# Samples' weighted sums as products of 256 columns, and a second quad in the planned entry of a feed-forward layer

## Chip, cores and metric

One core of a Trainium2 chip runs the whole program. The metric is device time in microseconds, the median of several executions. Engines are named as in the profile: PE (TensorE matmul) and PEld (its weight loads), DVE (VectorE), ACT (ScalarE), POOL (GpSimd), SP (SyncE, which issues the DMAs).

## The reference

A trunk of two layers runs over 1024 prompt rows and 64 sample rows (8 batches of 8 new tokens), width 1024. Layer 0 mixes tokens with a gated MLP, layer 1 with sliding-window attention; each is followed by a SwiGLU feed-forward layer of width 2816. The samples' attention reads cached keys and values:

```python
kk = jnp.concatenate([cache_k.astype(k_new.dtype), k_new], axis=1)
vv = jnp.concatenate([cache_v.astype(v_new.dtype), v_new], axis=1)
...
probs = sink_softmax(scores, sinks.reshape(N_KV_HEADS, Q_PER_KV))
out = jnp.einsum('bkgts,bskd->btkgd', probs.astype(vv.dtype), vv)
...
return (jax.nn.silu(h @ w_gate) * (h @ w_up)) @ w_down
```

For each sample batch b and key head k, 8 query heads x 8 tokens are weighted sums over 128 cached and 8 new value rows of 64 elements.

## The kernel before, in words

**Precision.** Large products run with each operand split into a high part (ACT copies it to the round format) and a low part (DVE subtracts), three matmuls per product: high x high, high x low, low x high. The samples' sums and all transposes use full-precision operands.

**Order of the work.** Two mechanisms set it. In the attention a `Flow` object keeps a modelled clock: `flow.pe(ns)` moves it on, `flow.later(ns, fn)` queues a step for a due time, and `flow.run()` runs what is due; the tile framework's own scheduler then orders the instructions of each engine at compile time. In a layer's entry (the second half of the output projection, the transposes of the normalised rows, and the first feed-forward products) a `Plan` takes tasks with costs from `TIME`, their dependencies and the buffers they take and give, places them by list scheduling, and writes them out under `manual_schedule`, so PE, ACT, DVE and POOL keep that order.

**Samples' attention** (class `Samples`, one instance per key head, at steps 19 and 31 of the 32 steps of the score loop). `scores` makes scores and softmax; 8460 ns later `probs` turns the probabilities by PE and masks them into `ptc` (cached keys) and `ptn` (new keys), 4 tiles j of 128 columns each; 1107 ns later `weigh` (lines 356 to 371) makes the sums. For each of 8 batches and two e it multiplies that batch's 64 value columns as weights with 32 probability columns (line 363), and the same for the new rows (line 364), into one "aux" bank of PSUM. Then ACT and DVE put the result into the attention rows (`put`, lines 2217, 627, 628) and the weights' slot is handed back (`W.done`). PSUM has 5 "bank" and 3 "aux" buffers.

**Around it.** The score loop also issues the query products (lines 621 to 623), the prompt's scores (2291, 2292), turns (2201), masks (2308, 2310) and sums (2324, 2326). Early parts of the output projection are begun for five row blocks, two inside the loop and three due 0, 1 and 2 us behind it (`begin`), each with a "bank" of its own, continued by `extend`, and finished in `project` (1005 to 1007), which releases the bank when `Enter.first` (1030, 1031) has read it.

**Feed-forward.** 22 column groups q (gate for even q, up for odd q) are computed by a seven-product scheme over 512-row halves. A quad of weights per q gives four units: `b1`, `b2` (loaded, scaled by ACT at line 465, split at 381 and 382) and `s1`, `s2` (sums of the raw quads by DVE, lines 401 to 404, then split). The steps per q: `p1` (b1), `p2` (b2), `p657` (products 6, 5 and 7 from s1, s2, s1, with the sums u2 at line 1499 and u3 at line 1507), the samples' side product (1452, 1453), `p4` and `p3`; all main products are lines 1373 to 1375. `take` adds a product to an earlier sum and applies Silu (even q) or multiplies into the gate rows and stores them (odd q). `p4` cannot start before u3 has been read out of its bank:

```python
part(s["b"], unit(q, "s1"), P, ent, "t3", False)
W.done(unit(q, "s1"))
u3 = s["u3"] = tmp()
nc.vector.tensor_tensor(u3, s["b"], s["keep"], op=ALU.add)
take(q, 1, 1, s["c"], u3)
```

`W.done` frees a unit, and `prepare` issues the next unit's preparation at once (at most 5 are live). Raw weights arrive by DMA into three buffers; a buffer is loaded anew when the low part that read it last has been issued.

**The planned entry** (`begin` inside `ffn`) covers the weights of quads 0 and 1 (`WORDER`, lines 1781 and 1785) and the steps of `MAIN`: p1 and p2 of q = 0 and 1, both side products, and products 6, 5, 7, 4, 3 of q = 0. The first half of quad 1's pair `b2` waits in the plan 3500 ns after the low part that frees its buffer. What follows runs in program order: `p657(1)`, `p1(2)`, `p4(1)`, `p3(1)`, then the loop over q = 2 to 21.

Of the kernel before, what the change touches and what calls it, by code (L numbers as in the profile page):

```python
# [19 lines left out]
P = 128  # L20
# [36 lines left out]
MAIN = ["1", "1'", "2", "2'", "6", "s", "5", "s'", "7", "4", "3"]  # L57
WORDER = [(0, "b1"), (0, "b2"), (1, "b1"), (0, "s1"), (0, "s2"), (1, "b2"), (1, "s1"), (1, "s2")]
K = {'sprobs': 8460, 'sweigh': 1107, 'xrows': 1607, 'tokw': 17761, 'var': 4147, 'centre': 4050, 'lnfin': 5018, 'mix0': 4469, 'mixc': 1659, 'mixn': 7044, 'mixt': 988, 'ln0': 1571, 'lnc': 6100, 'krow': 92, 'vrow': 2056, 'probs': 10000, 'weigh': 556, 'beg': 73, 'beg0': 0, 'ql': [159, 251], 'mp': [191, 253, 255, 255], 'ustep': 1.65, 'sat': [19, 31], 'cst0': 3015, 'cstep': 306, 'guest': [4, 7], 'lns': 47, 'sturn': 1300, 'rops': 9500, 'rstep': 550, 'zsum': 1500}
# [150 lines left out]
def trunk_kernel(ctx, tc, a):  # L210
# [86 lines left out]
    class Samples:  # L297
# [58 lines left out]
        def weigh(self, ptc, ptn):  # L356
            po = aux()
            for b in range(DB):
                for e in range(2):
                    j = 2 * (b // 4) + e  # L360
                    out = po[e * HD:(e + 1) * HD, b * 32:b * 32 + 32]
                    r = slice(b % 4 * 32, b % 4 * 32 + 32)
                    nc.tensor.matmul(out, self.cv[:, b, :], ptc[:, j, r], start=True, stop=False)
                    nc.tensor.matmul(out, self.vnew[:, b, :], ptn[:DS, j, r], start=False, stop=True)
            flow.pe(1500)
            pov = po[:, :256].rearrange("p (b f t) -> p b f t", b=DB, f=4)
            for i in range(4):
# [3 lines left out]
            W.done(self.slot)  # L371
# [1006 lines left out]
    def ffn(layer, ent, last, then=None):  # L1378
# [115 lines left out]
        def p657(q):  # L1494
            s = st[q]
            s["b"] = bank()
            part(s["b"], unit(q, "s1"), 0, ent, "t2", True)
            u2 = s["u2"] = tmp()
            nc.vector.tensor_tensor(u2, s["b"], s["keep"], op=ALU.add)
            flow.run()  # L1500
            s["c"] = bank()
            part(s["c"], unit(q, "s2"), P, ent, "t1", True)
            flow.run()
            part(s["b"], unit(q, "s1"), P, ent, "t3", False)
            W.done(unit(q, "s1"))
            u3 = s["u3"] = tmp()
            nc.vector.tensor_tensor(u3, s["b"], s["keep"], op=ALU.add)  # L1507
            take(q, 1, 1, s["c"], u3)

        def p4(q):  # L1510
            s = st[q]
            part(s["b"], unit(q, "b2"), P, ent, "t4", False)
            W.done(unit(q, "b2"))
            take(q, 1, 0, s["b"], s["keep"])

        def p3(q):
            s = st[q]
            part(s["c"], unit(q, "s2"), 0, ent, "y2", False)
            W.done(unit(q, "s2"))
            take(q, 0, 1, s["c"], s["u2"])  # L1520
# [248 lines left out]
        def begin():  # L1769
# [5 lines left out]
            def weights():  # L1775
# [96 lines left out]
            q, s, d = 0, st[0], {}  # L1872

            def six():
# [6 lines left out]
                d["u2"] = plan.add("DVE", TIME["tt"], u2, [(t, TIME["pe"])], take={"tmp": 1})  # L1881

            def five():
                d["5"] = product(q, "c", "s2", P, "t1", True)

            def seven():
                t = product(q, "b", "s1", P, "t3", False, [d["u2"]], True)
# [5 lines left out]
                d["u3"] = plan.add("DVE", TIME["tt"], u3, [(t, TIME["pe"])], take={"tmp": 1})  # L1893
                d["c"] = taken(d["5"], 1, 1, "c", "u3", [d["u3"]], {"tmp": 1})

            def taken(t, i, c, b, n, after, give):
                r = lambda: region(q, i, c)
                e = plan.add("DVE", TIME["tt"], lambda: nc.vector.tensor_tensor(r(), s[b], s[n], op=ALU.add),
                             [(t, TIME["pe"])] + after, give=give)
                plan.add("ACT", TIME["cp5"], lambda: nc.scalar.activation(r(), r(), AF.Silu), [e])  # L1900
                return e

            def four():
                t = product(q, "b", "b2", P, "t4", False, [d["u3"]], True)
                taken(t, 1, 0, "b", "keep", [], {"tmp": 1, "bank": 1})

            def three():
                t = product(q, "c", "s2", 0, "y2", False, [d["c"]], True)
                taken(t, 0, 1, "c", "u2", [], {"tmp": 1, "bank": 1})
# [3 lines left out]
            does = {"1": lambda: one(0), "1'": lambda: one(1), "2": lambda: two(0), "2'": lambda: two(1),  # L1913
                    "s": lambda: samples(0), "s'": lambda: samples(1), "6": six, "5": five, "7": seven, "4": four, "3": three}
            for n in MAIN:
                does[n]()
# [6 lines left out]
        steps = [(p657, 1), (p1, 2), (p4, 1), (p3, 1)]  # L1923
# [502 lines left out]
```

## Time and profile before

| | |
|---|---|
| median of 3 runs | 2144.86 us (2143.78 to 2147.54) |
| the profiled execution | 2147.14 us, its span 2145.1 us |
| mean granted TensorE clock | 0.991 of full speed |
| instructions | 29498 |

The page's first part gives each engine's busy time and its share of the span. A timeline row has the start, the time that the group covers, the engine, the line, the operation, output and inputs with their shapes (weights as 128*64, then the moving operand), and a count; in square brackets stands how long the engine was idle before it and what ended that. Matmuls are pipelined and their ends are modelled, so the time from one start to the next tells what a matmul costs, not its own duration. PEclk is the granted clock as a share of 2.4 GHz.

### The profile page before, as it was taken

How to read it: one execution, taken by the hardware profiler on the slowest of the kernel's cores; microseconds unless marked ns; L12 is line 12 of the kernel's file. 1: busy time of each engine (PE TensorE's matmuls, PEld its weight loads, DVE VectorE, ACT ScalarE, POOL GpSimd, SP SyncE). 2: the span in 40 equal slices, each digit the busy share in tenths (PEclk: the TensorE clock that was granted, in tenths of full speed). 3: DMA queues.
4: the chain of work that ended last, by engine and by line, in shares of the span. 5: the costliest groups of instructions: out<-in, count | busy, mean ns of one | idle time of the engine just before them, and what ended most of it. 6: DMA issues, size and time to landing. Idle time of an engine off the chain costs nothing.

```text
span 2145.1 us, 29498 instructions
## 1 busy us (share of the span) xinstructions
PE 2113.0 (99%) x11088; PEld 1810.7 (84%) x11088; DVE 1369.6 (64%) x2205; ACT 1044.5 (49%) x2096; POOL 167.9 (8%) x226
## 2 busy tenths in 40 slices
PE   8999999999999999999999999999999999999998
PEld 7999988788888888888899886888888888888886
DVE  5455457656665666566767766476666666665676
ACT  5234556444444433434567754474544444434342
POOL 1322211000000000000113221010000000000000
PEclk9999999999999999999999988999999999999999
DMA  4211233223332327767442111232323232277574
GB/s 146 63 47 29 89 112 104 80 91 97 99 96 84 106 95 280 255 195 231 128 121 54 43 38 53 90 137 75 100 80 101 95 100 83 88 250 276 181 255 147
DMA packets 176724, 257.12 MB, mean 120 GB/s; under 512 B 24659, under 2 KB 104773, under 8 KB 176582
## 3 DMA queue, kind: packets, MB, share of 16 engines
q1 hardware_dynamic: 176582, 255.24, 36.8%
q8 instruction: 87, 1.43, 0.3%
q14 instruction: 55, 0.45, 0.1%
HBM read 188.96 MB, written 60.62 MB: 116 GB/s over the span
## 4 chain that ended last, share of the span: by engine, by line
PE 91%; DVE 4%; ACT 2%; DMA 1%; issue 1%; POOL 0%; SPq 0%; DVEq 0%; POOLq 0%; ACTq 0%
PE bank L1599 14%; PE bank L1373 13%; PE bank L1374 12%; PE bank L1375 12%; PE bank L621 5%; PE bank L623 5%; PE bank L622 5%; PE aux L1599 4%; PE bank L1005 2%; PE bank L1007 2%; PE bank L1006 2%; PE bank L1452 2%; PE bank L1453 2%; PE aux L1607 2%; PE aux L1106 1%; PE aux L2324 1%
## 5 line engine op out<-in xcount | busy, mean ns | idle before, releaser
L1373 PE MATMUL bank<-act,act 128*128 128x512 f32 x1232 | 484.9, 394 | 3.9 <-DVE tmp L1507 3.9
L1374 PE MATMUL bank<-act,act 128*128 128x512 f32 x1232 | 482.8, 392 | 0.0
L1375 PE MATMUL bank<-act,act 128*128 128x512 f32 x1232 | 480.0, 390 | 0.0
L1599 PE MATMUL bank<-act,act 128*128 128x512 f32 x1452 | 341.2, 389 | 0.0
L382 DVE TENSOR_TENSOR act<-raw,act 128x1024 fp32r<-128x1024 f32 x197 | 241.6, 1228 | 128.1 <-ACT act L381 119.3
L1599 PEld LDWEIGHTS bank<-act,act 128*128 128x128 f32 x1452 | 272.4, 188 | 56.5
L381 ACT ACTIVATE act<-raw 128x1024 fp32r<-128x1024 f32 x197 | 208.3, 1059 | 218.1 <-PE bank L1453 75.5
L1373 PEld LDWEIGHTS bank<-act,act 128*128 128x128 f32 x1232 | 232.0, 188 | 50.0 <-DVE tmp L1507 4.7
L1375 PEld LDWEIGHTS bank<-act,act 128*128 128x128 f32 x1232 | 231.8, 188 | 49.1
L1374 PEld LDWEIGHTS bank<-act,act 128*128 128x128 f32 x1232 | 232.1, 188 | 43.6
L627 ACT ACTIVATE act<-act 128x1024 fp32r<-128x1024 f32 (+4 forms) x183 | 152.4, 882 | 174.5 <-PE aux L1599 64.8
L621 PE MATMUL bank<-act,act 128*128 128x384 f32 (+1 forms) x624 | 210.7, 338 | 2.0 <-DVE act L753 1.4
L623 PE MATMUL bank<-act,act 128*128 128x384 f32 (+1 forms) x624 | 207.5, 333 | 0.4 <-DVE act L382 0.4
L622 PE MATMUL bank<-act,act 128*128 128x384 f32 (+1 forms) x624 | 206.2, 331 | 0.7 <-DVE tok L978 0.7
L628 DVE TENSOR_TENSOR act<-act,act 128x1024 fp32r<-128x1024 f32 (+4 forms) x183 | 177.2, 1009 | 36.6 <-ACT act L627 25.9
L465 ACT ACTIVATE raw<-raw,vcol 128x256 f32<-128x256 f32 x352 | 152.1, 498 | 72.9 <-DMA raw<-in_f_w_up 44.7
L983 POOL TENSOR_TENSOR tok<-tok,expo 128x1 f32<-128x1 f32 (+1 forms) x63 | 38.4, 611 | 1604.8 <-DVE tok L978 1604.8
L621 PEld LDWEIGHTS bank<-act,act 128*128 128x128 f32 x624 | 118.8, 190 | 4.7 <-DVE act L753 1.6
L623 PEld LDWEIGHTS bank<-act,act 128*128 128x128 f32 x624 | 118.4, 190 | 2.1 <-issue 1.4
L622 PEld LDWEIGHTS bank<-act,act 128*128 128x128 f32 x624 | 118.8, 190 | 1.4 <-DVE tok L978 1.0
L1005 PE MATMUL bank<-act,act 128*128 128x512 f32 x256 | 102.2, 402 | 0.3 <-ACT act L627 0.3
L1007 PE MATMUL bank<-act,act 128*128 128x512 f32 x256 | 100.7, 398 | 0.0
(293 smaller groups left out, 3167.6 us busy)
## 6 DMA issues: line engine op xcount, KB each, us to landing
act<-in_f_w_down SPq DMA_DIRECT2D x90, 512.0 KB
raw<-in_f_w_gate SPq DMA_DIRECT2D x44, 512.0 KB
raw<-in_f_w_up SPq DMA_DIRECT2D x44, 512.0 KB
act<-hid_s SPq DMA_DIRECT2D x40, 512.0 KB
rows<-stream SPq DMA_DIRECT2D x24, 512.0 KB
hid_x<-rows SPq DMA_DIRECT2D x44, 256.0 KB
hid_s<-act SPq DMA_DIRECT2D x44, 256.0 KB
hid_s<-rows SPq DMA_DIRECT2D x44, 256.0 KB
```

What stands on the lines that cost most here:

```text
L381: nc.scalar.activation(self.hi, raw, AF.Copy)
L382: nc.vector.tensor_tensor(self.lo, raw, self.hi.bitcast(F32), op=ALU.subtract)
L465: nc.scalar.activation(v, v, AF.Copy, scale=col("f_norm_pre", e.gain[1] + j, e.gain[0]))
L621: nc.tensor.matmul(out[:, :n], h, xh[:, cs:cs + n], start=begin, stop=False)
L622: nc.tensor.matmul(out[:, :n], h, xl[:, cs:cs + n], start=False, stop=False)
L623: nc.tensor.matmul(out[:, :n], l, xh[:, cs:cs + n], start=False, stop=end)
L627: nc.scalar.activation(hi, src, AF.Copy)
L628: nc.vector.tensor_tensor(lo, src, hi.bitcast(F32), op=ALU.subtract)
L1373: nc.tensor.matmul(ps, h, xh, start=begin and k == 0, stop=False, skip_group_check=not begin)
L1374: nc.tensor.matmul(ps, h, xl, start=False, stop=False, skip_group_check=not begin)
L1375: nc.tensor.matmul(ps, l, xh, start=False, stop=k == 3, skip_group_check=not begin)
L1599: nc.tensor.matmul(ps, x, w, start=begin and e == k == 0, stop=end and e == n - 1 and k == 2, skip_group_check=adds)
```

## The change

Two parts. First, `weigh` makes, for each half of the batches and each e, one product with all 128 probability columns of a tile as weights and the values of four batches (256 columns) moving, and one for the new rows; ACT copies the four diagonal blocks out of PSUM, 2500 ns later two transposes bring them into the old layout, and the copies into the attention rows follow as before. Secondly, the plan of the entry takes in the rest of q = 1, the first product of q = 2 and the weights of quad 2. A third edit goes with it: `W.done` stands behind `take` in `p657`, `p4` and `p3`.

```diff
-MAIN = ["1", "1'", "2", "2'", "6", "s", "5", "s'", "7", "4", "3"]
-WORDER = [(0, "b1"), (0, "b2"), (1, "b1"), (0, "s1"), (0, "s2"), (1, "b2"), (1, "s1"), (1, "s2")]
+MAIN = ["1", "1'", "2", "2'", "6", "s", "5", "s'", "7", "4", "3", "6'", "5'", "7'", "1''", "4'", "3'"]
+WORDER = [(0, "b1"), (0, "b2"), (1, "b1"), (0, "s1"), (0, "s2"), (1, "b2"), (1, "s1"), (1, "s2"), (2, "b1"), (2, "b2"), (2, "s1"), (2, "s2")]
+RAWS = {(1, "b2"): (0, "s1"), (2, "b1"): (0, "s2"), (2, "b2"): (1, "s1")}
+K = {'sown': 2500, ...
...
         def weigh(self, ptc, ptn):
+            halves = []
+            for hb in range(2):
+                ps = bank()
+                for e in range(2):
+                    j, out = 2 * hb + e, ps[:, e * 256:(e + 1) * 256]
+                    v, vn = (t[:, 4 * hb:4 * hb + 4, :].rearrange("p b d -> p (b d)") for t in (self.cv, self.vnew))
+                    nc.tensor.matmul(out, ptc[:, j, :], v, start=True, stop=False)
+                    nc.tensor.matmul(out, ptn[:DS, j, :], vn, start=False, stop=True)
+                own = tmp([P, P])
+                for b in range(4):
+                    r = slice(b * 32, (b + 1) * 32)
+                    nc.scalar.activation(own[r, :].rearrange("p (e d) -> p e d", e=2),
+                                         ps[r, :].rearrange("p (e b d) -> p e b d", e=2, b=4)[:, :, b, :], AF.Copy)
+                halves.append(own)
+            flow.pe(2000)
+            W.done(self.slot)
+            flow.later(K["sown"], lambda: self.features(halves))
+
+        def features(self, halves):
             po = aux()
-            for b in range(DB):
-                for e in range(2):
-                    j = 2 * (b // 4) + e
-                    out = po[e * HD:(e + 1) * HD, b * 32:b * 32 + 32]
-                    r = slice(b % 4 * 32, b % 4 * 32 + 32)
-                    nc.tensor.matmul(out, self.cv[:, b, :], ptc[:, j, r], start=True, stop=False)
-                    nc.tensor.matmul(out, self.vnew[:, b, :], ptn[:DS, j, r], start=False, stop=True)
-            flow.pe(1500)
+            for hb in range(2):
+                nc.tensor.transpose(po[:, hb * P:(hb + 1) * P], halves[hb], ident)
+            flow.pe(220)
...
             part(s["b"], unit(q, "s1"), P, ent, "t3", False)
-            W.done(unit(q, "s1"))
             u3 = s["u3"] = tmp()
             nc.vector.tensor_tensor(u3, s["b"], s["keep"], op=ALU.add)
             take(q, 1, 1, s["c"], u3)
+            W.done(unit(q, "s1"))
...
                         a0 = plan.add("ACT", TIME["scale"], lambda box=box: (get(box), scale(box[0])),
-                                      [last, (lo[0, "s1"], 3500) if (q, n) == (1, "b2") else None])
+                                      [last, (lo[RAWS[key]], 3500) if key in RAWS else None])
...
+                e = plan.add("DVE", TIME["tt"], add, [(t, TIME["pe"])] + after, take={"tmp": 1}, give=give)
+                d[q, i, c] = plan.add("DVE", TIME["tt"], times, [e], take={"port": 1}, give={"port": 1, "tmp": 1})
...
+                if q == 1:
+                    plan.add("DVE", TIME["sums"], lambda: sums(1), [d[1, 1, 1], d[1, 1, 0], d[1, 0, 1], ev2[1]],
+                             take={"act": 1, "port": 1}, give={"port": 1})
...
-        steps = [(p657, 1), (p1, 2), (p4, 1), (p3, 1)]
+        steps = []
```

In `MAIN` one prime stands for q = 1 and two for q = 2. The step functions of the plan (`six`, `five`, `seven`, `four`, `three`, `taken`) now take q as an argument, and `taken` has the branch for odd q that adds, multiplies and stores.

## Rows read from the trace of the kernel before

**Rows 1.** The page, busy time of each engine

```profile
PE 2113.0 (99%) x11088; PEld 1810.7 (84%) x11088; DVE 1369.6 (64%) x2205; ACT 1044.5 (49%) x2096; POOL 167.9 (8%) x226
```

**Rows 2.** PE's waits over the span: waited for, us in total, times, longest

```profile
PE aux L2324 <- DVE act L2308: 4.1, 3, 2.8
PE bank L1373 <- DVE tmp L1507: 3.9, 2, 2.6
```

**Rows 3.** Views of lines 363 and 364: count, ns min/median/max, first and last start

```profile
L363 PE MATMUL aux<-sc,act x64: 222/294/316, 1241.0 to 1336.9; 128*64 128x32 f32 x64
...
L364 PE MATMUL aux<-act,act x64: 217/290/311, 1241.8 to 1337.2; 8*64 8x32 f32 x64
```

**Rows 4.** Stretch 1240 to 1250: us, PE, PEld, DVE, ACT, POOL busy, PEclk, DMA

```profile
1240.00:1250.00 10.00, 10.00 (x69) 8.18 (x67) 3.73 (x11) 3.97 (x13) 3.03 (x3) 0.69 0.09 22
```

**Rows 5.** Timeline of PE, first burst: start, us of the group, line, operation, count

```profile
1240.97 0.30 PE L363 MATMUL aux<-sc,act 128*64 128x32 f32 x2
1241.20 0.66 PE L323 MATMUL aux<-ident,raw 128*128 128x128 f32 x4
1241.79 0.30 PE L364 MATMUL aux<-act,act 8*64 8x32 f32 x2
...
1243.87 0.42 PE L363 MATMUL aux<-sc,act 128*64 128x32 f32 x2
...
1251.57 1.11 PE L323 MATMUL aux<-ident,raw 128*128 128x128 f32 x4
...
1257.44 0.32 PE L621 MATMUL bank<-act,act 128*128 128x320 f32 x1
```

**Rows 6.** Timeline of PE, second burst

```profile
1325.94 0.30 PE L363 MATMUL aux<-sc,act 128*64 128x32 f32 x2 [0.51 <-DVE sc L352]
1326.18 0.50 PE L1005 MATMUL bank<-act,act 128*128 128x512 f32 x1
...
1328.67 0.30 PE L364 MATMUL aux<-act,act 8*64 8x32 f32 x2
...
1337.46 0.80 PE L1007 MATMUL bank<-act,act 128*128 128x512 f32 x1
...
1342.83 0.63 PE L1007 MATMUL bank<-act,act 128*128 128x512 f32 x2
```

**Rows 7.** Timeline of PE, feed-forward entry of the first layer

```profile
396.49 0.39 PE L1374 MATMUL bank<-act,act 128*128 128x512 f32 x1
396.71 0.39 PE L1375 MATMUL bank<-act,act 128*128 128x512 f32 x1
399.68 0.50 PE L1373 MATMUL bank<-act,act 128*128 128x512 f32 x1 [2.57 <-DVE tmp L1507]
...
400.72 0.63 PE L1374 MATMUL bank<-act,act 128*128 128x512 f32 x1
...
404.12 0.39 PE L1373 MATMUL bank<-act,act 128*128 128x512 f32 x1
```

**Rows 8.** Timeline of PE, token mixing

```profile
189.99 1.50 PE L919 MATMUL aux<-act,tmp 128*128 128x128 f32 x12
191.25 0.42 PE L623 MATMUL bank<-act,act 128*128 128x384 f32 x1
```

**Rows 9.** Timeline of ACT, behind the first burst

```profile
1251.67 0.57 ACT L2217 ACTIVATE act<-aux 128x64 f32<-128x64 f32 x4
```

**Rows 10.** Timelines of ACT and DVE, feed-forward entry of the first layer

```profile
390.80 1.71 ACT L465 ACTIVATE raw<-raw,vcol 128x256 f32<-128x256 f32 x4 [4.61 <-DMA raw<-in_f_w_gate]
...
394.54 1.04 ACT L381 ACTIVATE act<-raw 128x1024 fp32r<-128x1024 f32 x1
...
395.61 1.23 DVE L382 TENSOR_TENSOR act<-raw,act 128x1024 fp32r<-128x1024 f32 x1 [5.49 <-ACT act L381]
...
398.94 0.68 DVE L1507 TENSOR_TENSOR tmp<-bank,tmp 128x512 f32<-128x512 f32 x1
```

**Rows 11.** Timeline of PE, feed-forward entry of the second layer

```profile
1479.18 0.50 PE L1373 MATMUL bank<-act,act 128*128 128x512 f32 x1 [1.32 <-DVE tmp L1507]
```

More of the change, by code (lines that the diff above doesn't have):

```diff
@@ L1512, in p4 @@
             part(s["b"], unit(q, "b2"), P, ent, "t4", False)
+            take(q, 1, 0, s["b"], s["keep"])
             W.done(unit(q, "b2"))
-            take(q, 1, 0, s["b"], s["keep"])
         def p3(q):
@@ L1518, in p3 @@
             part(s["c"], unit(q, "s2"), 0, ent, "y2", False)
+            take(q, 0, 1, s["c"], s["u2"])
             W.done(unit(q, "s2"))
-            take(q, 0, 1, s["c"], s["u2"])
             if q % 2:
@@ L1879, in u2, with five, seven @@
                     nc.vector.tensor_tensor(s["u2"], s["b"], s["keep"], op=ALU.add)
[L1881 to L1887, printed above, removed]
+                d[q, "u2"] = plan.add("DVE", TIME["tt"], u2, [(t, TIME["pe"])], take={"tmp": 1})
+            def five(q):
+                d[q, "5"] = product(q, "c", "s2", P, "t1", True)
+            def seven(q):
+                s = st[q]
+                t = product(q, "b", "s1", P, "t3", False, [d[q, "u2"]], True)
                 def u3():
@@ L1891, in u3 @@
                     nc.vector.tensor_tensor(s["u3"], s["b"], s["keep"], op=ALU.add)
[L1893 to L1900, printed above, removed]
-                return e
@@ L1903, in four @@
[L1903 to L1909, printed above, removed]
+                d[q, "u3"] = plan.add("DVE", TIME["tt"], u3, [(t, TIME["pe"])], take={"tmp": 1})
+                d[q, "c"] = taken(q, d[q, "5"], 1, 1, "c", "u3", [d[q, "u3"]], {"tmp": 1})
@@ new lines, in taken, with add, times @@
+            def taken(q, t, i, c, b, n, after, give):
+                s, r = st[q], lambda: region(q, i, c)
+                if q == 0:
+                    e = plan.add("DVE", TIME["tt"], lambda: nc.vector.tensor_tensor(r(), s[b], s[n], op=ALU.add),
+                                 [(t, TIME["pe"])] + after, give=give)
+                    plan.add("ACT", TIME["cp5"], lambda: nc.scalar.activation(r(), r(), AF.Silu), [e])
+                    return e
+                v = {}
+                def add():
+                    v["t"] = tmp()
+                    nc.vector.tensor_tensor(v["t"], s[b], s[n], op=ALU.add)
+                def times():
+                    nc.vector.tensor_tensor(r(), v["t"], r(), op=ALU.mult)
+                    store(q, i, c)
+                e = plan.add("DVE", TIME["tt"], add, [(t, TIME["pe"])] + after, take={"tmp": 1}, give=give)
+                d[q, i, c] = plan.add("DVE", TIME["tt"], times, [e], take={"port": 1}, give={"port": 1, "tmp": 1})
+                return e
@@ new lines, in four, with three @@
+            def four(q):
+                t = product(q, "b", "b2", P, "t4", False, [d[q, "u3"]], True)
+                taken(q, t, 1, 0, "b", "keep", [], {"tmp": 1, "bank": 1})
+            def three(q):
+                t = product(q, "c", "s2", 0, "y2", False, [d[q, "c"]], True)
+                taken(q, t, 0, 1, "c", "u2", [], {"tmp": 1, "bank": 1})
+                if q == 1:
+                    plan.add("DVE", TIME["sums"], lambda: sums(1), [d[1, 1, 1], d[1, 1, 0], d[1, 0, 1], ev2[1]],
+                             take={"act": 1, "port": 1}, give={"port": 1})
@@ L1911, in begin @@
             kept, ev2 = {}, {}
             weights()
-            does = {"1": lambda: one(0), "1'": lambda: one(1), "2": lambda: two(0), "2'": lambda: two(1),
-                    "s": lambda: samples(0), "s'": lambda: samples(1), "6": six, "5": five, "7": seven, "4": four, "3": three}
+            does = {"1": one, "2": two, "s": samples, "6": six, "5": five, "7": seven, "4": four, "3": three}
             for n in MAIN:
-                does[n]()
+                does[n[0]](n.count("'"))
             with tc.manual_schedule(engines={PE, mybir.EngineType.Activation, mybir.EngineType.DVE, mybir.EngineType.Pool}):
```

8 lines of the change are left out of this document (4 added, 4 removed).

## The prediction

> **What bounds the kernel now.** I read the page first: PE is busy 99% of the span [rows 1], so only work taken off PE, a wait of PE, or clock given back can shorten it. Then PE's waits over the whole span: they sum to little, and the two largest are the attention's turned probabilities waiting for DVE (4.1 us) and the second weight pair of the feed-forward entry waiting for DVE (3.9 us in two pieces, one per layer) [rows 2]. The change touches the second of these and, in the attention, the samples' weighted sums. So I read three stretches.
>
> The sums' products (lines 363 and 364) are 64 instructions each, over two key heads: 32 columns moving against 64 columns of weights [rows 3]. A full-precision product is two instructions (2 x 16 products of each line, 64 instructions), so each head has 64 instructions in all. In the ten microseconds of the first burst the granted clock is 0.69 [rows 4], that is a mixture of the two levels, 2.4 and 1.2 GHz. The timeline shows where it falls: nine pairs from 1241.79 to 1243.87, 0.23 us each, then 22 pairs to 1251.57, 0.35 each, with no wait named; the matmuls behind them stay slow until 1257.44 [rows 5]. The second head does the same: a pair at 1325.94, then ten other matmuls from 1326.18, the rest from 1328.67 to 1337.46, and the clock back at 1342.83 [rows 6].
>
> At the feed-forward entry of the first layer PE issues its last ready matmul at 396.71 and the next at 399.68, then runs at half rate from 400.72 to 404.12, eight matmuls [rows 7].
>
> **The sums, step by step.** What goes: first head 1251.57 - 1240.97 = 10.60 us, less the four transposes from 1241.20 to 1241.79 (0.59) that stand inside [rows 5], 10.0 us. Second head 0.24 + (1337.46 - 1328.67) = 9.03 us [rows 6]. Together 19.0 us.
>
> What comes, per head: two halves x two e x two operands = 8 products of 256 columns against 128 columns of weights, so 16 instructions. The trace has no such product. The nearest is the token mixing (line 919): full precision, 128 x 128 weights, 128 columns, 12 instructions from 189.99 to 191.25, 0.105 us each [rows 8]. Twice the columns: 0.21 us. Lower bound 0.105 (columns free up to 256); upper bound the 0.43 that 0.21 becomes at the low clock. I take 0.21, since the row is of the same precision and width and was not slowed. 16 x 0.21 = 3.4 us, and two transposes at the rate of the four above, 0.3: 3.7 us a head, 7.4 for both. Net -11.6 us. Between the bounds it is 3.4 us more, or 6.9 less.
>
> The slow tails: eight matmuls took 3.40 us between 400.72 and 404.12 [rows 7], 0.425 each, against 0.22 to 0.23 at full rate (the step from 396.49 to 396.71), so 0.466 of a slow stretch is loss. The stretches behind the bursts last 5.87 us [rows 5] and 5.37 us [rows 6]: 2.7 + 2.5 = 5.2 us. If the long products hold the clock, as line 919's do, these come back; if not, none. I take all.
>
> The copies of diagonal blocks are new on ACT: 8 per head, 32 partitions x 128 elements. The nearest row has four copies of 128 x 64 in 0.57 us, 0.14 each [rows 9]; with up to twice that, 1.1 to 2.2 us of ACT per head. ACT is busy 3.97 of 10 us while the first burst runs [rows 4], so they cost nothing unless the transposes, planned 2500 ns later, come up before them; then PE waits, at most 2 us a head. I put 0.5 each. The feature copies behind the transposes are the old ones, later by that delay; only the last block of the output projection reads the second head's, and the slot of weights is handed back before them, not after.
>
> The products now take two of the five "bank" buffers, where they took an "aux". For the second head the code matters: the five early sums of the output projection are begun within 2 us of the end of the score loop and hold all five banks; the second head's products are due 9.6 us after its scores. They must stand behind the projection's first two blocks, which free banks. Lower bound nothing (that stage is dense matmuls), upper bound one evacuation for each half, about 2 us each. I put 1 us. Sum for this part: -11.6 - 5.2 + 1 + 1 = -14.8 us; without the add-backs -16.8.
>
> **The second quad in the planned entry.** What is late now: the third sum of quad 1 (line 1507), which PE needs for its next step, starts on DVE at 398.94. DVE stood 5.49 us until ACT's split at 394.54 let it take the low part at 395.61; between that one's end and 398.94 lie 2.1 us, three of the four weight sums (lines 401 to 403, 0.7 each) [rows 10]. ACT had scaled the weights at 390.80, after 4.61 us of waiting for their DMA, and did 2.0 us of other work before the split. PE was ready at 396.94 (396.71 and one step) and started at 399.68: 2.74 us, and 3.40 x 0.466 = 1.6 us of slow clock [rows 7]: 4.3 us. In the second layer the same wait is 1.3 to 1.5 us [rows 11], with no slow stretch. The whole prize is 5.8 us.
>
> The written-out order now puts scale, split, low part and sums of quad 2 in with quad 1's steps. It supposes 3.5 us between the buffer's release and the scale; here the DMA is what ACT waits for, so the scale stays at 390.80. If the split follows at once: 392.5, low part 393.5, four sums of 0.7 until 397.5 (by the plan's costs they are ready before line 1507, so they go first), line 1507 until 398.2. PE then waits 1.3 us, too short to lose the clock, going by the second layer's wait, behind which none was lost. Gain 1.4 + 1.6 = 3.0 in the first layer; in the second the same 1.4 covers nearly all of its wait. I take 4.4 us. Bounds: 5.8, and -1.2 (the split stays late and the fourth sum too goes ahead of line 1507: 0.6 a layer).
>
> The scale of quad 2's first half moves on ACT behind the splits of quad 1: 1.7 us, inside the 4.61 us that ACT waits anyway [rows 10]; with that cover gone it would delay the split by as much. Loads are issued from the same low parts; the stores of quad 1 and its sums are the same DMAs, in the new order on SP. No PE work is added.
>
> Handing units back after the evacuation rather than before it, in 20 quads of each layer, moves weight preparation behind one DVE sum (0.68 us, line 1507 [rows 10]). Among all 18 rows of PE's waits the feed-forward lines have only the one shown [rows 2], so none for weights, and I cost it at nothing; rival D is its price.
>
> **Sum.** -14.8 - 4.4 = -19.2, say -20, as the 0.5 us that PE waited ahead of the second burst may go too. The profiled run took 2147.1 us with a span of 2145.1, 2.3 above the median of 2144.86. Against its own time 2127; against the median **2125**.
>
> **Rivals.** (A) *The plan gains nothing*: the split stays late behind automatic ACT work, and the wait stands or grows. For it: the order is made from costs that have the DMA faster than here. Time: 2144.9 - 14.8 + 0 to 1.2 = 2130.
>
> (B) *The long products do not hold the clock.* Half of them have 8 rows of contraction only, as line 364 has, and the bursts that fell have them. Then 2 x (16 x 0.43 + 0.6) = 15 us in place of 19, the tails stay, and the plan gives 4.4: 2136. Against it: line 919 at full rate.
>
> (C) *The attention turns to DVE.* PE's largest wait is there for DVE already [rows 2]; work that PE reaches sooner queues on DVE. Half of 16.8 is lost: 2133. Against it: DVE is busy 3.73 of 10 us during the burst [rows 4], so it idles because of it.
>
> (D) *Slower: the weights' supply in the feed-forward loop.* Each hand-back waits for an evacuation, and with every buffer in use the split of the next unit does too. If PE then waits 0.68 us in each of 40 quads, that is 27 us: 2152. It decides from 0.5 us a quad (20 / 40). Against it: scaling and splitting run on ACT, which does not wait for that sum, and nothing in 40 quads waits for weights now.
>
> (E) *No change: the columns count.* By line 919 a column costs 0.82 ns, 32 of them 0.026 us, and the old 64 instructions 1.7 us a head; the new ones 3.4. If the other 8 us are waiting that stays, the change costs 3.4 us in the sums and gains 4.4: 2144. Against it: no releaser is named inside the bursts, and a pair costs 0.23 us just as a pair of four times the columns does, so the cost goes with the instruction. The Trainium skill, "TensorE: Matmul & The Clock Gate", section "Back-to-back issue gap", states the rule that speaks for this rival: the gap is N / 2.4 ns plus 2.5. By it, as an estimate, 64 instructions of 32 columns take 1.0 us and 16 of 256 columns 1.7. The trace disagrees for the small ones: 0.115 us each, not 0.016.
>
> That the change does not do what it says is possible only in the order that the schedulers choose; that is A.
>
> **Chances.** Forecast 0.60 (own range 2120 to 2129), A 0.16, B 0.07, C 0.10, D 0.04, E 0.03. A measurement of this kernel tells 0.2%, 4.3 us, from no change. Faster: forecast, A, B, C: 0.93. Same: E, 0.03. Slower: D, 0.04. Range: down to 2118 for products at the lower bound and the whole prize (20 + 3.4 + 1.4 + half of the add-backs), up to 2134, which takes in A and C and leaves out B, D and E.
>
> **What would show it.** Right: 16 instructions of 256 columns a head about 0.21 us apart, granted clock 1.00 around them; line 1507's wait gone or under 1.3 us in each layer, no slow stretch there; the feed-forward loops as long as before. Wrong: products 0.4 us apart (B); PE waits on DVE in the attention well over 4.1 us (C); the planned order's first step after line 1507 waits over 2.7 us (A); waits for low parts in the loops (D).

## The result, and the profile after

The changed kernel takes 2130.81 us (median of 6 runs, 2126.55 to 2133.64), the kernel before in the same company 2145.92 (2140.95 to 2147.74): ratio 0.993, 95% interval 0.9913 to 0.9948, or 15.1 us less. Forecast were 2125 and -20. The stated range, 2118 to 2134, holds it; the forecast's own range, 2120 to 2129, does not, and it lies at the 2130 of rival A. The profiled execution took 2133.59 us, 13.5 less than the one shown of before.

The page (span; busy time of each engine) beside [rows 1]:

```profile
span 2131.6 us, 29327 instructions
...
PE 2098.7 (98%) x10996; PEld 1797.8 (84%) x10996; DVE 1370.7 (64%) x2205; ACT 1048.1 (49%) x2112; POOL 167.1 (8%) x226
```

PE's waits over the span, the lines for the three places that matter, beside [rows 2]:

```profile
PE aux L702 <- DMA act<-in_x_prompt: 4.8, 4, 2.3
PE aux L702 <- DVE act L643: 3.7, 2, 2.9
PE aux L2357 <- DVE act L2341: 3.5, 3, 2.1
...
PE bank L1388 <- ACT act L1796: 2.3, 2, 1.3
```

PE's busy time fell by 14.3 us (2113.0 less 2098.7), about the whole gain. The attention's wait for DVE (line 2357, the old 2324) is 3.5 us where it was 4.1, and the entry's (line 1388, the old 1373) is 2.3 where it was 3.9. The two waits on line 702 (the old 687) are the program's opening, which the change doesn't touch.

The first head's burst on PE's timeline, beside [rows 5], and four rows around the second's, beside [rows 6]:

```profile
1241.82 1.03 PE L365 MATMUL bank<-act,sc 128*128 128x256 f32 x4
1242.68 0.60 PE L324 MATMUL aux<-ident,raw 128*128 128x128 f32 x4
1243.21 0.69 PE L366 MATMUL bank<-act,act 8*128 8x256 f32 x2
1243.84 0.70 PE L365 MATMUL bank<-act,sc 128*128 128x256 f32 x2
1244.47 1.12 PE L366 MATMUL bank<-act,act 8*128 8x256 f32 x4
1245.52 0.70 PE L365 MATMUL bank<-act,sc 128*128 128x256 f32 x2
1246.15 0.69 PE L366 MATMUL bank<-act,act 8*128 8x256 f32 x2
1246.78 0.65 PE L2234 MATMUL aux<-ident,sc 128*128 128x128 f32 x4
...
1334.88 0.59 PE L365 MATMUL bank<-act,sc 128*128 128x256 f32 x2
1335.40 0.69 PE L366 MATMUL bank<-act,act 8*128 8x256 f32 x2
...
1339.16 0.69 PE L366 MATMUL bank<-act,act 8*128 8x256 f32 x2
1339.79 0.50 PE L1022 MATMUL bank<-act,act 128*128 128x512 f32 x1
```

A group of 2 is one product. From 1241.82 to 1246.78 lie 4.96 us, 0.53 of them transposes: 4.4 us for the eight products. The steps differ: two products of 128 rows in a row take 0.86 us, 0.43 each; a product behind one of the other height takes 0.63 (1243.21 to 1243.84); two of 8 rows in a row take 1.05 (1244.47 to 1245.52), 0.63 and 0.42. The second head alternates throughout and takes 4.9 us, from 1334.88 to 1339.79; no wait stands in front of it. The granted clock (last but two) of the first burst, against 0.69 in [rows 4], and of a stretch with a wait on DVE of 2.1 us in it:

```profile
1240.00:1250.00 10.00, 10.00 (x60) 7.68 (x58) 7.27 (x17) 8.47 (x31) 3.25 (x4) 1.00 0.26 75
...
1300.00:1310.00 10.00, 9.44 (x39) 7.61 (x40) 7.76 (x26) 5.82 (x30) 3.63 (x4) 0.66 0.02 7
```

The feed-forward entry of the first layer on PE's timeline, beside [rows 7]:

```profile
401.12 0.39 PE L1390 MATMUL bank<-act,act 128*128 128x512 f32 x1
402.86 0.50 PE L1388 MATMUL bank<-act,act 128*128 128x512 f32 x1 [1.35 <-ACT act L1796]
```

The same stretch on ACT's timeline, and then on DVE's, beside [rows 10]:

```profile
392.75 1.70 ACT L480 ACTIVATE raw<-raw,vcol 128x256 f32<-128x256 f32 x4
395.56 1.71 ACT L480 ACTIVATE raw<-raw,vcol 128x256 f32<-128x256 f32 x4 [1.11 <-DMA raw<-in_f_w_up]
397.18 1.04 ACT L1796 ACTIVATE act<-raw 128x1024 fp32r<-128x1024 f32 x1
```

```profile
398.25 1.23 DVE L1800 TENSOR_TENSOR act<-raw,act 128x1024 fp32r<-128x1024 f32 x1 [4.17 <-ACT act L1796]
...
401.69 0.69 DVE L419 TENSOR_TENSOR raw<-raw,raw 128x512 f32<-128x512 f32 x1
402.30 0.68 DVE L1908 TENSOR_TENSOR tmp<-bank,tmp 128x512 f32<-128x512 f32 x1
```

Line 1908 is the planned form of 1507, the third sum. PE's wait is 1.5 us (402.86 less 401.35, when it was ready) where it was 2.74, and no slow clock follows. The row names ACT's split, but that had come at 397.18; by the times, what ends last is the third sum, behind the last of the four weight sums (419). The split itself stands behind a scale (395.56) of weights that the plan doesn't know: quad 3's.

### The profile page after: what moved, and what is told of

Same layout as the page of the kernel before. It is cut to its first block, busy times and chain, and to the rows that moved or that the text cites. A ratio compares the mean times of both kernels' runs of the same rounds, so it can differ in the third digit from the quotient of the medians.

```text
span 2131.6 us, 29327 instructions
## 1 busy us (share of the span) xinstructions
PE 2098.7 (98%) x10996; PEld 1797.8 (84%) x10996; DVE 1370.7 (64%) x2205; ACT 1048.1 (49%) x2112; POOL 167.1 (8%) x226
## 4 chain that ended last, share of the span: by engine, by line
PE 93%; DVE 4%; ACT 2%; DMA 1%; issue 0%; POOL 0%; SPq 0%; DVEq 0%; POOLq 0%; ACTq 0%
PE bank L1614 15%; PE bank L1388 13%; PE bank L1389 13%; PE bank L1390 13%; PE bank L636 5%; PE bank L638 5%; PE bank L637 5%; PE aux L1614 4%; PE bank L1020 3%; PE bank L1022 3%; PE bank L1021 3%; PE bank L1468 2%; PE bank L1467 2%; PE aux L1622 2%; PE aux L1121 1%; PE aux L2359 1%
## 5 line engine op out<-in xcount | busy, mean ns | idle before, releaser
L1389 PE MATMUL bank<-act,act 128*128 128x512 f32 x1232 | 482.4, 392 | 0.0
L397 DVE TENSOR_TENSOR act<-raw,act 128x1024 fp32r<-128x1024 f32 x189 | 233.4, 1236 | 126.4 <-ACT act L396 117.3
L396 ACT ACTIVATE act<-raw 128x1024 fp32r<-128x1024 f32 x189 | 199.8, 1058 | 205.1 <-PE bank L1468 71.1
```

Source lines behind the costliest of these rows:

```text
L396: nc.scalar.activation(self.hi, raw, AF.Copy)
L397: nc.vector.tensor_tensor(self.lo, raw, self.hi.bitcast(F32), op=ALU.subtract)
L1389: nc.tensor.matmul(ps, h, xl, start=False, stop=False, skip_group_check=not begin)
```

## The experiments

Eleven kernels besides a repeat of the changed one. Each is compared with the kernel before on the same chip.

**e1, the sums alone.** The new `weigh` and `features` in the kernel before.

> Only the samples' weighted sums are changed; the planned entry and the hand-backs are as before. Theory: the attention gives back 14.8 us, as the two profiles have it between the first matmul of the attention's projections and the end of the output projection, and the opening of the program, whose order of instructions is the same, varies from run to run by 4 to 5 us. So the ratio to before is 0.993 (-14.8 of 2146), the stretch from the first matmul of the query products to the last of the output projection is 14 to 16 us shorter, and nothing else moves beyond the opening. Rival 1 (the opening is made longer by the new sums): ratio 0.995, with the token mixing again starting at 195 us. Rival 2 (the slow clock behind the bursts was not the bursts' doing): only 11 us, 0.995, with stretches at a low clock left behind the products.

Measured: 2133.62 us, ratio 0.9943 (0.993 to 0.9956), -11.5 us (here and below, the difference of the medians).

**e2, the plan alone.** The changed kernel with `weigh` of before:

```diff
...
-                    nc.tensor.matmul(out, ptc[:, j, :], v, start=True, stop=False)
-                    nc.tensor.matmul(out, ptn[:DS, j, :], vn, start=False, stop=True)
+                    nc.tensor.matmul(out, self.cv[:, b, :], ptc[:, j, r], start=True, stop=False)
+                    nc.tensor.matmul(out, self.vnew[:, b, :], ptn[:DS, j, r], start=False, stop=True)
...
```

> The planned entry with two pairs of quads and the later hand-backs, with the weighted sums of before. Theory: the first layer's entry gives 3.0 us, the second's 0.3, so the ratio is 0.9985 (-3.3), which times can hardly tell from 1; the profile shows a wait of 1.3 to 1.5 us in the first layer with no slow clock behind it, and about 0.9 us in the second. The forecast's own size was -4.4 (0.998). Rival (the plan makes the opening longer): ratio 1.000 to 1.001, the token mixing again at 195 us.

Measured: 2141.56 us, ratio 0.9985 (0.9976 to 0.9994), -3.6 us.

**e3, the hand-backs alone.**

```diff
             part(s["b"], unit(q, "b2"), P, ent, "t4", False)
-            W.done(unit(q, "b2"))
             take(q, 1, 0, s["b"], s["keep"])
+            W.done(unit(q, "b2"))
```

(and the same in `p657` and `p3`).

> Only the three hand-backs of the weights' units are moved behind the evacuation of the sum; order of instructions as before on every engine. Theory: nothing, ratio 0.998 to 1.002, no wait of PE for weights in the feed-forward loops. Rival D at its full price: 40 quads by 0.68 us, +27 us, ratio 1.013; a tenth of it, 1.001, would be out of sight in the time but seen as waits of PE on lines of the feed-forward products.

Measured: 2144.32 us, ratio 0.9999 (0.999 to 1.0007), and no wait for weights in the loops. Rival D is out.

**e4, the changed kernel again.**

> The changed kernel once more, in the same company. Theory: the opening's 4.5 to 5.3 us of the profiled run are a matter of the run, not of the kernel; so over the kernels of this job the token mixing starts anywhere from 189 to 196 us, and the ratio is 0.9915 to 0.993 (-18.1 at the most, as the two profiles have it behind the opening). Rival: the opening belongs to the changed kernel: the token mixing starts at 195 us or later here, and no earlier than that in the kernel that has the part responsible.

Measured: 2128.34 us, ratio 0.9925 (0.9909 to 0.994), -16.8 us; its token mixing starts at 190.0.

Six profiles now give the stages, from the first and last starts in the views of lines (numbered here as in the kernel before): the opening up to the first token mixing (919); the first and the last feed-forward product of layer 1 (1373); from the first transpose at the attention's entry (1351) to the last at the second feed-forward entry (1106); from there to the last down product (1599). The stretches between agree within 0.9 us.

| us | opening | feed-forward 1 | attention | rest |
|---|---|---|---|---|
| before | 190.0 | 487.0 | 403.6 | 674.1 |
| e2, plan alone | 190.6 | 484.6 | 400.7 | 674.2 |
| e3, hand-backs alone | 194.2 | 486.7 | 401.3 | 674.3 |
| e1, sums alone | 189.7 | 486.5 | 388.7 | 674.1 |
| after | 195.3 | 484.1 | 388.8 | 673.7 |
| e4, after again | 190.0 | 484.4 | 388.4 | 674.0 |

Three things follow. First, the opening is a matter of the run: the order of instructions there is the same on every engine in all six, and it starts the token mixing at 195.3 in one profile of the changed kernel and at 190.0 in the other. The view of its line in e3, which has the old sums and the old plan:

```profile
L919 PE MATMUL aux<-act,tmp x128: 269/275/276, 194.2 to 273.1; 128*128 128x128 f32 x128
```

Secondly, the plan is worth 2.4 us in the first layer (mean of three with it, 484.4, against 486.7 without) and 0.2 in the second. Thirdly, the sums are worth 13.2 us (mean of 403.6, 400.7 and 401.3, less that of 388.7, 388.8 and 388.4); by the two profiles first compared it was 14.8. The old products lose more or less clock from run to run. In e2, with the same short products, the first burst's windows read:

```profile
1240.00:1250.00 10.00, 10.00 (x71) 8.49 (x69) 2.26 (x6) 4.06 (x18) 1.96 (x2) 0.72 0.09 22
1250.00:1260.00 10.00, 10.00 (x77) 8.66 (x76) 6.95 (x18) 5.15 (x19) 1.90 (x2) 0.94 0.18 54
```

In the profile of before the second of these windows has 0.63. Summed over both bursts, one less the granted clock, times the window, comes to 11.9 us in the profile of before, 6.8 in e2, 8.5 in e3, and nothing in the two profiles of the changed kernel. (The time lost is less than that: an old pair takes 0.35 us at the low clock against 0.23, one and a half times as long and not twice.)

The new products don't always keep the clock, though. In three of the five profiles that have them (after, e1, e4, and e7 and e8 below) PE fell to the low clock right behind one of the two bursts, and here, in the order e1 (second burst), e7 (first), e8 (second), are these windows of PE, with the granted clock last but two:

```profile
1330.00:1340.00 10.00, 10.00 (x33) 0.83 0.47 162
1240.00:1250.00 10.00, 10.00 (x71) 0.83 0.14 44
1320.00:1330.00 10.00, 10.00 (x46) 0.83 0.80 259
```

Taken in windows of 2 us the clock goes down to 0.50 (1336 to 1338 in e1, 1242 to 1244 in e7, 1322 to 1324 in e8), and each place comes to 1.7 us by the same count.

**e5 and e6, the same columns in shorter products.** Why is a long product cheaper? The changed kernel with each product cut:

```diff
-                    nc.tensor.matmul(out, ptc[:, j, :], v, start=True, stop=False)
-                    nc.tensor.matmul(out, ptn[:DS, j, :], vn, start=False, stop=True)
+                    for c in range(0, 256, 32):
+                        nc.tensor.matmul(out[:, c:c + 32], ptc[:, j, :], v[:, c:c + 32], start=True, stop=False)
+                        nc.tensor.matmul(out[:, c:c + 32], ptn[:DS, j, :], vn[:, c:c + 32], start=False, stop=True)
```

> The changed kernel with each product of 256 columns issued as eight of 32 columns: the same weights, the same columns in all, eight times the instructions (128 a head in place of 16). Theory (a short product costs by the instruction, about 0.105 to 0.115 us, and its burst loses the clock): the burst takes 13.4 to 14.7 us a head at full clock in place of 3.4, so +20 to +23 us for both heads, and 3 to 7 us a head more where the granted clock falls; in all 26 to 37 us over the changed kernel, ratio to before 1.005 to 1.010. Rival E (the columns count): the same 3.4 us a head, ratio 0.9925 as the changed kernel. In between, the instructions cost 0.115 us but the clock stays at 1.00: +20 to +23, ratio 1.002 to 1.003.

> The changed kernel with each product of 256 columns issued as two of 128: 32 instructions a head, the same columns. Theory: 0.105 us each as in the token mixing, so 3.4 us a head as before, no loss of clock, ratio 0.9925 (0 against the changed kernel). Rival (each instruction has a price of its own beside its columns): up to 0.21 us each, +3.4 us a head, ratio 0.9955.

Measured: pieces of 32 take 2189.05 us, ratio 1.0206 (1.0193 to 1.022), far over every number given, with the granted clock at 0.50 from 1250 to 1270; pieces of 128 (steps of 128 in place of 32) 2138.1 us, ratio 0.9965 (0.9951 to 0.9978), near the rival, though part of that is clock (0.55 from 1240 to 1250). Two neighbouring products of e5's timeline at full clock, two at the low one, and two of e6:

```profile
1239.54 0.40 PE L367 MATMUL bank<-act,act 8*128 8x32 f32 x2
1239.88 0.41 PE L366 MATMUL bank<-act,sc 128*128 128x32 f32 x2
...
1254.96 0.63 PE L367 MATMUL bank<-act,act 8*128 8x32 f32 x2
1255.52 0.64 PE L366 MATMUL bank<-act,sc 128*128 128x32 f32 x2
```

```profile
1236.34 0.49 PE L366 MATMUL bank<-act,sc 128*128 128x128 f32 x2
1236.76 0.48 PE L367 MATMUL bank<-act,act 8*128 8x128 f32 x2
```

A product of 32, 128 and 256 columns costs 0.34, 0.42 and 0.63 us. Neither a price by columns nor one of 0.105 us an instruction gives these, and 0.42 for 128 columns (two instructions) is twice what line 919 pays [rows 8]. What line 919 has not is a neighbour of another height: here 128 rows and 8 rows alternate. The weight loads show it in the changed kernel repeated (e4, timeline of PEld):

```profile
1237.70 0.29 PEld L366 LDWEIGHTS bank<-act,act 8*128 8x128 f32 x2 [0.17 <-issue]
1238.33 0.30 PEld L365 LDWEIGHTS bank<-act,sc 128*128 128x128 f32 x2 [0.33 <-issue]
1238.96 0.72 PEld L366 LDWEIGHTS bank<-act,act 8*128 8x128 f32 x4 [0.33 <-issue]
```

In front of each group of the other height the loads stand still, 0.33 us (0.17 at the first, behind transposes), with nothing that they are seen to wait for.

**e9, no change of height.** The new theory's own test:

```diff
-                    nc.tensor.matmul(out, ptn[:DS, j, :], vn, start=False, stop=True)
+                    nc.tensor.matmul(out, ptc[:, j, :], v, start=False, stop=True)
```

> The changed kernel with the eight-row products (the samples' new keys) replaced by a second copy of the 128-row ones: the same number of instructions and columns, but no change of contraction height between products. What is left out: the new keys' share of the sums; the cached keys' share is counted twice. Theory (a change of height between neighbouring products keeps the next weights from loading under the running product): each product of 256 columns costs 0.42 us throughout, where the changed kernel has 0.63 behind a change of height and 0.42 behind a product of the same height; so a head's products take 3.4 us in place of 4.4 to 5.0, -2.6 us in all, ratio to before 0.991. Rival (each product has a fixed price of 0.2 us beside its columns): 0.63 as before, ratio 0.9925.

Measured: 2125.61 us, ratio 0.9912 (0.9898 to 0.9927). The new keys' share is left out, so this kernel's sums are not the program's. The timeline (the last row but one is the eighth and last product):

```profile
1241.16 0.60 PE L365 MATMUL bank<-act,sc 128*128 128x256 f32 x2
1241.60 0.59 PE L366 MATMUL bank<-act,sc 128*128 128x256 f32 x2
...
1244.19 0.59 PE L366 MATMUL bank<-act,sc 128*128 128x256 f32 x2
1244.62 0.60 PE L324 MATMUL aux<-ident,raw 128*128 128x128 f32 x4
```

0.43 us a product, eight in 3.46: the 0.20 us (0.63 less 0.43) go with the change of height, not with the product. Here each pair also repeats its weights and columns; the first two products of the changed kernel, and e11 below, have 0.43 with different ones.

**e10, the old products by height.** The kernel before with nothing changed but the order of `weigh`:

```diff
-            for b in range(DB):
-                for e in range(2):
...
-                    nc.tensor.matmul(out, self.cv[:, b, :], ptc[:, j, r], start=True, stop=False)
-                    nc.tensor.matmul(out, self.vnew[:, b, :], ptn[:DS, j, r], start=False, stop=True)
+            for t, w in ((self.cv, ptc), (self.vnew, ptn[:DS])):
+                for b in range(DB):
+                    for e in range(2):
...
+                        nc.tensor.matmul(out, t[:, b, :], w[:, 2 * (b // 4) + e, b % 4 * 32:b % 4 * 32 + 32],
+                                         start=t is self.cv and b == 0, stop=t is not self.cv and b == DB - 1,
+                                         skip_group_check=True)
```

> The kernel before with its short products reordered alone: all 16 products of the cached keys (128 rows), then all 16 of the new keys (8 rows), one change of height a head in place of 31. Theory (the change of height is what a short product costs): 0.23 us a product falls to 0.10 to 0.13 (two instructions of 0.05 to 0.06, as the interleaved 64-column products behind the projections run), so a head's 32 products take 3.2 to 4.2 us in place of 7.4 at full clock, and with the shorter burst the slow clock shrinks or goes: -6 to -15 us, ratio 0.993 to 0.997. Rival (the cost goes with the instruction, as the forecast had it): 0.23 us stays, ratio 1.000.

Measured: 2128.76 us, ratio 0.9922 (0.9907 to 0.9937): with the old plan, no less than the new sums alone give (e1, 0.9943); the attention stage is 385.7 us, e1's 388.7. The first head's burst:

```profile
1241.64 1.12 PE L362 MATMUL aux<-sc,act 128*64 128x32 f32 x32
1242.69 1.12 PE L362 MATMUL aux<-act,act 8*64 8x32 f32 x32
1243.74 1.09 PE L323 MATMUL aux<-ident,raw 128*128 128x128 f32 x8
```

The 64 instructions that took 10.0 us (7.4 at the 0.23 a pair of full clock) take 2.1, 0.033 each, below the bounds that the expectation gave, and the granted clock is 1.00 in every window around both bursts (1230 to 1250 and 1315 to 1325).

**e7, the split first.** The plan gets one more step, the scaling of quad 3's first weights behind the split of quad 2's second pair:

```diff
...
+                    if key == (2, "b2"):
+                        split = h
...
+                plan.add("ACT", TIME["scale"], ahead, [split, (lo[1, "s2"], 3500)])
```

> The changed kernel with one more step in the planned order: the scaling of the third quad pair's first weights (quad 3, first half) stands in the plan behind the split of quad 2's second half, so that it cannot go ahead of it. Theory (rest of the wait at the entry: ACT scales weights for which it waits on DMA ahead of the split, so the low part, the four sums and the third sum of quad 1 are late): the split starts some 2.7 us earlier in the first layer, the four sums are through before PE needs the third sum, and PE's wait of 1.5 to 1.7 us there falls to under 0.4; in the second layer 0.9 us falls likewise. Ratio to the changed kernel 0.9988 (-2.5 us), against before 0.991 to 0.992. Rival (the split waits for a buffer that PE frees, not for ACT): the wait stands within 0.3 us, ratio as the changed kernel.

Measured: 2123.49 us, ratio 0.9898 (0.9884 to 0.9911), and in PE's waits line 1388 is gone, in both layers. ACT's timeline at the first entry:

```profile
388.79 1.71 ACT L480 ACTIVATE raw<-raw,vcol 128x256 f32<-128x256 f32 x4
390.54 1.06 ACT L1796 ACTIVATE act<-raw 128x1024 fp32r<-128x1024 f32 x1
391.71 1.71 ACT L480 ACTIVATE raw<-raw,vcol 128x256 f32<-128x256 f32 x4
```

and the third sum on DVE's:

```profile
395.68 0.68 DVE L1918 TENSOR_TENSOR tmp<-bank,tmp 128x512 f32<-128x512 f32 x1
```

The split now stands 1.75 us behind its scale, where it stood 4.43, and the third sum is done at 396.36, a microsecond before PE gets to the step that needs it (397.36, without idle time). The feed-forward stages are 482.4 and 672.4 us against the changed kernel's 484.1 to 484.4 and 673.7 to 674.0, some 3.3 us less in both.

**e8, the buffers.**

```diff
-                ps = bank()
+                ps = aux()
```

> The changed kernel with the long products in the buffers named aux, as the short ones had them, in place of bank. Theory: the second head's products no longer wait for the output projection's first two blocks; they go ahead of them, as in the kernel before, and PE gains at most the 1 us that the forecast had put down for this: ratio 0.992 to 0.9925. Rival (the wait for banks had cost the second head as much as 5 us, by which its stretch shrank less than the first one's): ratio 0.990. Other rival (behind the last scores PE has nothing else and the early products are waited for): a wait on DVE in front of them, ratio 0.993 to 0.994.

Measured: 2128.52 us, ratio 0.9928 (0.9916 to 0.9941), the changed kernel's own. The second head's products moved from 1334.88 to 1316.39, ahead of the projection, and nothing was gained: the attention stage is 390.3 us, 1.7 of it the clock lost behind that burst. PE's other waits moved too (a new one of 1.7 us for DVE at line 1020, and 1.8 in place of 3.5 at line 2357). That the banks cost nothing is read from this together with the changed kernel's own rows, which have no wait in front of 1334.88.

**e11 and e12, both mended.** e11 is e7 with the long products by height as far as the banks allow; e12 is e7 with e10's `weigh` in place of the long products. e11's edit:

```diff
-            for hb in range(2):
-                ps = bank()
...
-                    nc.tensor.matmul(out, ptc[:, j, :], v, start=True, stop=False)
-                    nc.tensor.matmul(out, ptn[:DS, j, :], vn, start=False, stop=True)
+            halves, banks = [], [bank(), bank()]
+            for t, w in ((self.cv, ptc), (self.vnew, ptn[:DS])):
+                for j in range(4):
...
+                    nc.tensor.matmul(banks[j // 2][:, j % 2 * 256:(j % 2 + 1) * 256], w[:, j, :], v,
+                                     start=t is self.cv and j % 2 == 0, stop=t is not self.cv and j % 2 == 1,
+                                     skip_group_check=True)
```

> The changed kernel with the third pair's scaling behind the split (as in the earlier run) and its long products ordered by height where the banks allow: four of 128 rows, then four of 8 rows in the first head; two and two in the second, where one bank comes free after the other. Theory: the earlier run's 0.990 and some 1.6 us more, 0.989; in the first head the products take 3.6 us in place of 4.4, in the second 4.2 in place of 5.0. Rival (both banks held longer keep the projection's blocks waiting): 0.990 or more, with a wait for banks behind the products.

> The planned entry with the third pair's scaling behind the split, and in the attention the short products of the kernel before, ordered by height, with no copies of blocks and no transposes. Theory: the gains add, -17 of the reordering and -6 of the entries (4.5 in the first layer, 1.7 in the second): -23 us, ratio 0.989; each head's 32 products take 2.1 us in place of 3.4 for long ones of equal height, so it is no slower than the best version with long products (0.9888) and needs none of their copies. Rival (the earlier slot of the second head's products, in front of the projection, costs a wait on DVE that the long ones hide): 0.990 to 0.991.

Measured: e11 2120.57 us, ratio 0.9888 (0.9871 to 0.9904); e12 2120.17 us, ratio 0.9878 (0.9861 to 0.9894), 24.6 us below before. No difference between the two can be told, and both beat the changed kernel. e11's first head has four products of 128 rows, each with weights of its own, in 1.73 us, 0.43 each:

```profile
1232.96 1.89 PE L363 MATMUL bank<-act,sc 128*128 128x256 f32 x8
1234.69 0.60 PE L324 MATMUL aux<-ident,raw 128*128 128x128 f32 x4
```

e12 needs neither copies of blocks nor transposes of sums. Its 32 products of a head, 16 of each height, in the window of the first burst (ns, first and last start):

```profile
L363 PE MATMUL aux<-sc,act x32: 222/223/243, 1235.0 to 1235.9; 128*64 128x32 f32 x32
L363 PE MATMUL aux<-act,act x32: 217/218/239, 1236.0 to 1236.9; 8*64 8x32 f32 x32
```

## Why the forecast was right, and where its sizes were off

**The sums' direction and size held; a price did not.** "Twice the columns: 0.21 us" an instruction, 3.4 us a head, came out as 4.4 and 4.9. The row chosen [rows 8] had the shape and the precision, but not the neighbour of another height. The two add-backs of 1 us, for the transposes and for the banks, came to nothing: PE's waits in the changed kernel have none for either. So +2.5 and -2 nearly cancelled, by luck, and that the profiled pair shows just the -14.8 of the forecast is luck as well: over three profiles of either kind it is -13.2.

**"The cost goes with the instruction" was wrong.** This was said against rival E. In e10 the same instructions cost 0.033 us in place of 0.115: E was right that columns and instructions are cheap, and wrong that the rest is waiting that stays. It is the change of height, 31 times a head before and seven times at the most after. The Trainium skill, "TensorEngine Tiling (Array Packing)", section "Key Properties", states that a change of tiling mode drains TensorE; no run here shows that a product of 8 rows is such a mode, but the 0.20 us of a change, and the loads that stand still, would agree with it. The Trainium skill, "TensorE: Matmul & The Clock Gate", section "Back-to-back issue gap", has a floor of about 25 ns for up to 64 columns, which the forecast's estimate by that section left out; e10's 33 ns is near it. The forecast set the trace against that section's rule, and what it read there was the price of the change of height.

**Clock was the larger part of the gain, by an estimate.** From the rows, at full clock the old products take 14.7 us for both heads (0.23 a pair), the new ones 9.3, and four transposes some 0.8 (line 380, 0.19 us each), so that 4.6 of the 13.2 us are cheaper products. The rest is for the most part clock, inside the old bursts and behind them. The forecast had the tails behind them at 5.2 us from one profile. They came back in both profiles of the changed kernel, but that "the long products hold the clock" is not so in every run: in e1, e7 and e8 it was lost behind them, 1.7 us each by the count above. So rival B is out as a whole, since products cost 0.63 us at the most and most of the clock is kept, but its reason held in 3 of 10 bursts. Alternating products of 32 and of 128 columns lost more. The eight bursts of e9 to e12, with no or few changes of height, lost nothing; that this comes of the order is likely, and eight bursts don't show it.

**The plan, -4.4, gave 2.6**, and its two steps were both off. "The scale stays at 390.80" was wrong: set back by the 4.5 us by which this run's feed-forward layer starts later, 392.75 is 388.25, for ACT no longer waits for that DMA. "If the split follows at once" was wrong too: quad 3's scale, with 1.1 us of waiting for its own DMA, went in between. Net, 402.30 is 397.8 against 398.94: the third sum comes 1.1 us sooner where 1.4 was forecast, and the clock's 1.6 came back. In the second layer 1.4 was forecast and 0.2 measured. Rival A has the right reason for what is missing, a split that stays late behind automatic ACT work: e7, which takes that work out of the way, gains about 3.3 us. Its outcome, a plan that gains nothing, did not come, though the measured time lies at its 2130 (the repeat's 2128.34 lies in the forecast's own range).

**The hand-backs, nothing**: e3. **Rival C**: PE's wait for DVE in the attention is 3.5 us, not above 4.1. The slow clock around the waits there, between 1290 and 1320, is 3.4 us by the same count in this profile and 1.7 in that of before, but over the profiles it goes from nothing (e1, e7) to 3.4 (e3 with the old sums, e4 with the new), so no gain or loss of the change is read from it.

**The sum.** Forecast -20; by the stages -13.2 - 2.4 - 0.2 = -15.8, and by medians -15.1 and -16.8. Of the missing 4.2 us, 1.8 are the plan's, 1.6 the sums', in part because the old bursts were sized in a profile that had lost more clock than others, and 0.8 were added to the sum for a wait of 0.5 us and by rounding. The profiled pair's 13.5 has an opening in it that was 5.3 us longer by chance. The terms given for the range's lower end add up to 2119, not 2118.

## What to carry to other kernels

Before short products are rebuilt into long ones, look at what stands between them: here products of 128 and of 8 rows in turn, and sorting them by height gave at least as much as the rebuilding. Take the price of a new product from a row with the same neighbours, not only the same shape. A written order rules only over what is in it: work that the framework's scheduler adds on the same engine, here the scaling of the next weights, goes between its steps unless it is made a step itself. And size a loss of clock over several profiles, and count a kernel as keeping the clock only after several.

## What was not expected of the hardware

A change of contraction height, from 128 rows to 8 or back, between neighbouring full-precision products costs 0.16 to 0.21 us at 2.4 GHz: 0.63 against 0.43 at 256 columns, 0.42 against twice line 919's 0.105 at 128, and 0.23 against 0.066 at 32 columns with 64 columns of weights. A full-precision instruction of 32 columns with 64 columns of weights costs 0.033 us where the height stays. In the opening, the same order of instructions brings PE to the token mixing at 189.5 to 195.3 us over the 14 profiles of this study; where it came at 195.3, PE had waited 3.7 us for DVE, 2.9 of them up to 30, and the granted clock from 30 to 35 was 0.66.
